# Three buffers for weight casts and residues, 4 KB runs for the up rows, and one reading of the routing table for two steps, in a hybrid decoder layer

## The chip, the cores and the metric

The kernel runs on one core of one Trainium2 chip. A core has a matrix engine (TensorE, PE in the profile; its weight loads are listed apart as PEld), a vector engine (VectorE, DVE), a scalar engine (ScalarE, ACT), GpSimd (POOL) and a queue engine (SyncE, SP). Each takes its instructions strictly in the order in which the program was built. Sixteen DMA engines move data between memory (HBM) and the on-chip buffer. The metric is the device time of one execution in microseconds (us).

## The reference, cut to what matters

One layer over 1,024 tokens of width 1,024, all in float32. First a mixer: a gated short convolution and a dilated sliding-window attention, merged by sigmoid gates. Then a retrieval of experts ("PEER"), which is most of the work:

```python
u   = rms_norm(h, norm_ffn)
q   = (u @ w_query).reshape(T, 8, 2, 128)
s   = einsum('thcd,hckd->thck', q, sub_keys)
top_s, top_i = top_k(s, 16)
...
best_s, pos = top_k(cand_s, 16)
idx   = take_along_axis(cand_i, pos, axis=-1)
gates = softmax(best_s)
...
a   = gelu(einsum('cd,ced->ce', xc, expert_down[ic]))
y   = einsum('ce,ced->cd', gc * a, expert_up[ic])
out = rms_norm(h + y, final_norm)
```

Each token picks 8 x 16 = 128 of 16,384 experts. An expert is one row of `expert_down` (for its activation) and one row of `expert_up` (what it adds).

## The kernel before, in words

Tokens stand in eight tiles of 128. The first four tiles ("half 0") go through the mixer first, then the other four ("half 1").

Tiles 0 to 3 get their experts by gathering (`experts`, the "side" work): for each of the 128 picks GpSimd issues an indirect DMA that fetches 128 rows of 4 KB (L873 from `down`, L889 from `up`), into one of four buffers `row`, and VectorE takes a dot product with the token's vector (L875) or adds the weighted row to a sum (L891). Tile 1 leaves out its `up` part, so there are 512 gathers on L873 and 384 on L889.

Tiles 4 to 7, and the `up` part of tile 1, are done densely on TensorE (`dense`): all 16,384 experts are computed in 32 groups of 512, and a routing table `g_d` in memory holds each token's gate for each expert (zero for those not picked).

- `hidden(q)`, for a group: four chunks of `down_t` go through `weights`, `project` multiplies each with the tokens, ScalarE applies Gelu (L913) into a buffer `ga` of 1 MB. Groups below `STORED` write `ga` to memory (`a_d`) and `fetch` it later; `HOLD` = 4 groups keep it on the chip.
- `build` makes the routing table: VectorE and ScalarE write one-hot matrices `oa` and `ob`, TensorE multiplies them into `psg` (L975), ScalarE copies that into `stg` (L977), and SP stores it (L981). One call covers 128 tokens.
- `weigh(q)`: loads the group's gates `gg` from `g_d` (and `gx` for tile 1), multiplies `ga` by them (L990) and splits the product into `hh` and `hl`.
- The last loop takes the groups in `order`: it loads four pieces `rawu` of the `up` rows, splits each into `uh` and `ul` (L181, L182), and multiplies. Six of ten output pieces stay in PSUM through the whole loop (`held`); the other four go through `psu` and are added to `rest` (L1089).

Every float32 product is done as three products of rounded numbers (`mm3`): a number is split into `hi` (a cast, on ScalarE) and `lo` (the residue, on VectorE), and TensorE computes hi*hi, hi*lo and lo*hi. `weights` (L161) does this for a chunk of 512 KB: a DMA into `raw`, the cast at L165 into `hi`, the residue at L167 into `lo`; `raw` has `RAWS` buffers, `hi` and `lo` have `HILO` each.

The order of the work: `main` runs the mixer of half 1 and then `dense`, both as generators that yield estimated costs; for each cost that it yields, so much of the side work is emitted, and within the first part of `dense` so much of the building of the table. A scheduler then orders each engine's instructions from readiness and that order. When the table is done, the builder's pool is closed, and the buffers of the last loop (pool `up_p`, with `uu`) take its place on the chip.

Of the kernel before, what the change touches and what calls it, by code (L numbers as in the profile page):

```python
# [8 lines left out]
F32 = mybir.dt.float32  # L9
# [4 lines left out]
ALU = mybir.AluOpType  # L14
# [3 lines left out]
P = 128  # L18
T = 1024
TH = 512  # L20
# [11 lines left out]
TC = 32  # L32
NB = 4
# [1 line left out]
PACE_D = 2.0  # L35
PACE_C = 2.2
RATE_G = 0.8
STORED = 27
HOLD = 4
RAWS = 4  # L40
HILO = 2
SUBS = ((1, 2), (1, 1))
OBUF = 4
GATES = 4
# [19 lines left out]

@with_exitstack
def hybrid_layer(ctx, tc, x, xT, pos, rotc, norm_mix, w_proj, w_v, conv_w, w_conv_out, w_attn_out,
                 gate_bias, w_out, norm_ffn, w_query, sub_keys, down, down_t, up, final_norm, out):
    nc = tc.nc
    V, S, G, PE = nc.vector, nc.scalar, nc.gpsimd, nc.tensor
    SIDE = getattr(nc, QUEUE)  # L70
# [2 lines left out]
    m8 = ctx.enter_context(tc.tile_pool(name="m8", bufs=BIGS))  # L73
    wp = ctx.enter_context(tc.tile_pool(name="wp", bufs=2))
    gt = ctx.enter_context(tc.tile_pool(name="gt", bufs=ROWS))
    ex = ctx.enter_context(tc.tile_pool(name="ex", bufs=1))
# [74 lines left out]
    s_d = dram.tile([3, P, 16, P], F32, name="s_d")  # L151
    a_d = dram.tile([STORED, P, NB, TH], F32, name="a_d")
    g_d = dram.tile([(TH + len(XT) * P) // TC, P, P, TC], F32, name="g_d")
# [26 lines left out]
    def split(hi, lo, src):  # L180
        S.copy(hi, src)  # L181
        V.tensor_tensor(lo, src, hi.bitcast(F32), op=ALU.subtract)  # L182
# [573 lines left out]
    def choose(column, last, picks):  # L756
# [50 lines left out]
        other = ex.tile([P, 16, 16], F32, tag="wk", bufs=1, name="other")  # L807
        for k in range(16):
            into = (found, other)[k % 2]
            wk = ex.tile([P, 16, 16], F32, tag="wq", bufs=2, name="wq") if k > 1 else into  # L810
            V.scalar_tensor_tensor(wk, where, float(k), names[:, :, k:k + 1].to_broadcast([P, 16, 16]),
                                   op0=ALU.is_equal, op1=ALU.mult)
            if k > 1:
                V.tensor_tensor(into, into, wk, op=ALU.add)
            if k % 2:
                yield 0.7
        V.tensor_tensor(found, found, other, op=ALU.add)
        gs = ex.tile([P, 8], F32, tag="gs", name="gs")
        ge = ex.tile([P, 8, 16], F32, tag="ge", bufs=GATES + 2, name="ge")
        V.tensor_tensor(ge, best, best[:, :, 0:1].to_broadcast([P, 8, 16]), op=ALU.subtract)  # L820
        S.activation(ge, ge, AF.Exp)
        V.tensor_reduce(gs, ge, AX.X, ALU.add)
# [77 lines left out]
    def dense():  # L900
# [8 lines left out]
        def hidden(q):  # L909
            ga = big("ga")  # L910
            for ii in range(NB):
                ps = project(weights(down_t[NB * q + ii]), U2)
                S.activation(ga[:, ii], ps, AF.Gelu)  # L913
                yield 5.3
            if q < STORED:
                nc.sync.dma_start(a_d[q], ga)
# [31 lines left out]
        def build(srcs, c0):  # L948
# [5 lines left out]
                for c in range(c0, c0 + P // TC):  # L954
# [25 lines left out]
                    for w in range(4):  # L980
                        nc.sync.dma_start(g_d[c, :, 32 * w:32 * w + 32], stg[w])  # L981

        def weigh(q):
            gg = m8.tile([P, TH // TC, NB, TC], F32, tag="big", name="gg")
            nc.sync.dma_start(gg, g_d[:TH // TC, :, NB * q:NB * q + NB].rearrange("c j i t -> j c i t"))
            ga = gas.pop(q)
            hh, hl = bigr("hh"), bigr("hl")
            for ii in range(NB):
                v = ga[:, ii].rearrange("p (c t) -> p c t", t=TC)
                V.tensor_tensor(v, v, gg[:, :, ii], op=ALU.mult)  # L990
                split(hh[:, ii], hl[:, ii], ga[:, ii])
            parts = [(hh[:, :, tt * P:tt * P + P], hl[:, :, tt * P:tt * P + P]) for tt in range(4)]
            for k in range(len(XT)):
                gx = up_p.tile([P, P // TC, NB, TC], F32, tag="gx", bufs=GXB, name="gx")
                c0 = (TH + k * P) // TC
                nc.sync.dma_start(gx, g_d[c0:c0 + P // TC, :, NB * q:NB * q + NB].rearrange("c j i t -> j c i t"))
                xh = up_p.tile([P, NB, P], F32R, tag="xh", bufs=XHB, name="xh")
                xl = up_p.tile([P, NB, P], F32R, tag="xl", bufs=XHB, name="xl")
                view = [t.rearrange("p i (c t) -> p c i t", t=TC) for t in (xh, xl)]
                S.copy(view[0], gx)  # L1000
                V.tensor_tensor(view[1], gx, view[0].bitcast(F32), op=ALU.subtract)
                parts.append((xh, xl))
            return parts
# [8 lines left out]
        for q in list(range(STORED)) + first:  # L1012
            for c in hidden(q):
                yield c / PACE_C
                debt += c * RATE_G
                while debt > 0:
                    k = next(builder, None)
# [16 lines left out]
        for n_q, q in enumerate(order):  # L1034
# [22 lines left out]
            for n in range(2):  # L1057
                uu = []
                whole = [bigr("uh_end"), bigr("ul_end")] if end and n else None
                for ii in range(0, NB, 2):  # L1060
                    raw = wp.tile([P, 2, TH], F32, tag="raw", bufs=RAWS, name="rawu")
                    r0 = (NB * q + ii) * P
                    nc.sync.dma_start(raw, up[r0:r0 + 2 * P, n * TH:n * TH + TH].rearrange("(a p) d -> p a d", a=2))
                    if whole:
                        uh, ul = (t[:, ii:ii + 2] for t in whole)
                    else:
                        uh = up_p.tile([P, 2, TH], F32R, tag="uu", bufs=UPS, name="uh")
                        ul = up_p.tile([P, 2, TH], F32R, tag="uu", bufs=UPS, name="ul")
                    split(uh, ul, raw)
                    uu.append((uh, ul))  # L1070
                for some in [[tt] for tt in range(NT)] if end and n else rounds[n]:
# [10 lines left out]
                    for tt in some:  # L1082
                        ps = acc[tt]
                        if (n, tt) in rest and not end:
                            d = rest[n, tt]
# [4 lines left out]
                        if end:  # L1090
                            st = sts[:, tt]
                            d = tokrow(h1, tt)[:, n * TH:n * TH + TH]
# [3 lines left out]
                        if end and n:  # L1096
                            V.tensor_tensor(st[:, 0:1], st[:, 0:1], st[:, 3:4], op=ALU.add)
                            r0 = TILES[tt] * P
# [14 lines left out]
    for step in main():  # L1113
        due += step
        while due > 0:
            k = next(side, None)
# [59 lines left out]
```

## Time and profile before

| | |
|---|---|
| median of 3 timed runs | 3423.3 us (3423.22 to 3426.72) |
| the profiled execution | 3433.88 us |
| its span, first to last instruction | 3432.1 us |
| PE busy | 3274.4 us (95%) |
| DVE busy | 2760.1 us (80%) |
| ACT busy | 1461.7 us (43%) |
| POOL busy | 1190.2 us (35%) |
| moved by DMA | 948.08 MB, 276 GB/s mean |

A span's busy share is a mean over stages with different limits; the stretches of the span are read one by one further down. The profiled execution is 10.6 us longer than the median of the timed runs. "Idle before" an instruction, and what ended it, is inferred from semaphore events. The full matmul has 512 columns.

### The profile page before, as it was taken

The page shows a single profiled execution, that of the slowest core. Times are in us where ns is not written, and L with a number is a line of the kernel's source. Part 1 is how long each engine was busy: PE and PEld are TensorE (multiplying, and loading weights), DVE is VectorE, ACT ScalarE, POOL GpSimd, SP SyncE. Part 2 cuts the span into 40 slices and gives each one's busy share as a digit, 9 for nine tenths or more (in the row PEclk, how much of TensorE's full clock was granted, in tenths as well). Part 3 has the DMA queues.
Part 4 walks back from the last instruction along what each step waited for, and adds up shares of the span by engine and source line. Part 5 has one row for each costly group of instructions (what it writes and reads, how often), then busy time and mean ns, then how long its engine had stood idle before and what let it go on. Part 6 is the DMA issues. An engine that isn't in the chain of part 4 may idle for free.

```text
span 3432.1 us, 47074 instructions
## 1 busy us (share of the span) xinstructions
PE 3274.4 (95%) x15923; PEld 2685.0 (78%) x15923; DVE 2760.1 (80%) x5646; ACT 1461.7 (43%) x3271; POOL 1190.2 (35%) x944
## 2 busy tenths in 40 slices
PE   7999999999989999988999989999999999999998
PEld 6787888887767777767777878888877878787787
DVE  4333355689999889988999999998887878888887
ACT  3544444443334353333226777787632222222222
POOL 0000000014543345555434443464544334444342
PEclk9999999999989999989999999999999999999999
DMA  4233335668888678988889898999989989999895
GB/s 129 77 119 110 103 127 191 244 230 305 302 279 276 227 260 307 342 316 292 315 316 328 329 330 334 344 340 336 348 301 336 334 316 338 326 340 333 309 350 208
DMA packets 364307, 948.08 MB, mean 276 GB/s; under 512 B 33952, under 2 KB 127648, under 8 KB 356640
## 3 DMA queue, kind: packets, MB, share of 16 engines
q1 hardware_dynamic: 232016, 465.27, 38.9%
q0 software_dynamic: 132048, 479.78, 38.8%
q8 instruction: 126, 2.06, 0.2%
q14 instruction: 117, 0.96, 0.1%
HBM read 843.15 MB, written 95.49 MB: 273 GB/s over the span
## 4 chain that ended last, share of the span: by engine, by line
PE 32%; DVE 20%; DMA 14%; issue 11%; POOL 5%; ACT 1%; SPq 0%; DVEq 0%; POOLq 0%; ACTq 0%
DVE row L875 6%; PE ps L178 6%; PE ps L176 6%; PE ps L177 6%; DMA row<-in_down,idx 5%; DMA rowu<-in_up,idx 4%; DMA gg<-g_d 4%; DVE lo L167 3%; POOL row L873 3%; POOL rowu L889 2%; PE held L177 2%; PE held L178 2%; PE held L176 2%; DVE acc L891 1%; PE psg L975 1%
## 5 line engine op out<-in xcount | busy, mean ns | idle before, releaser
L873 POOL DMA_INDIRECT row<-in_down,idx x512 | 640.9, 1252 | 885.2 <-DVE a L875 465.6
L889 POOL DMA_INDIRECT rowu<-in_up,idx x384 | 525.8, 1369 | 621.1 <-DVE acc L891 499.0
L165 ACT CAST hi<-raw 128x1024 fp32r<-128x1024 f32 x368 | 387.6, 1053 | 746.0 <-PE ps L177 541.1
L875 DVE CUSTOM_DVE_ANT_0 row<-row,ut 128x1024 f32<-128x1024 f32 x512 | 618.8, 1215 | 79.2 <-DMA row<-in_down,idx 74.0
L167 DVE TENSOR_TENSOR lo<-raw,hi 128x1024 fp32r<-128x1024 f32 x368 | 448.1, 1218 | 247.9 <-ACT hi L165 238.6
L178 PE MATMUL ps<-vhi,lo 128*128 128x512 f32 (+1 forms) x1408 | 535.4, 382 | 33.5 <-DVE lo L167 33.4
L176 PE MATMUL ps<-vhi,hi 128*128 128x512 f32 (+1 forms) x1408 | 530.6, 377 | 10.8 <-ACT hi L165 6.7
L891 DVE SCALAR_TENSOR_TENSOR acc<-rowu,a,acc 128x1024 f32<-128x1024 f32 x384 | 491.2, 1279 | 59.7 <-DMA rowu<-in_up,idx 57.3
L177 PE MATMUL ps<-vlo,hi 128*128 128x512 f32 (+1 forms) x1408 | 528.9, 376 | 0.0
L178 PE MATMUL ps<-uhi,lo 128*128 128x512 f32 x1024 | 409.1, 400 | 4.2 <-DVE lo L167 4.2
L176 PE MATMUL ps<-uhi,hi 128*128 128x512 f32 x1024 | 407.6, 399 | 5.7 <-ACT uhi L181 3.1
L177 PE MATMUL ps<-ulo,hi 128*128 128x512 f32 x1024 | 409.1, 400 | 0.5 <-DVE ulo L182 0.5
L178 PEld LDWEIGHTS ps<-vhi,lo 128*128 128x128 f32 x1408 | 269.1, 191 | 87.4 <-DVE lo L167 44.4
L176 PEld LDWEIGHTS ps<-vhi,hi 128*128 128x128 f32 x1408 | 269.7, 192 | 58.9 <-ACT hi L165 10.9
L177 PEld LDWEIGHTS ps<-vlo,hi 128*128 128x128 f32 x1408 | 269.1, 191 | 45.1
L177 PE MATMUL held<-ul,hh 128*128 128x512 f32 x624 | 247.0, 396 | 11.1 <-DVE ul L182 10.9
L178 PE MATMUL held<-uh,hl 128*128 128x512 f32 x624 | 244.0, 392 | 2.5 <-DVE hl L182 2.5
L176 PEld LDWEIGHTS ps<-uhi,hi 128*128 128x128 f32 x1024 | 194.1, 190 | 52.1 <-ACT uhi L181 5.2
L176 PE MATMUL held<-uh,hh 128*128 128x512 f32 x624 | 233.3, 393 | 0.0
L178 PEld LDWEIGHTS ps<-uhi,lo 128*128 128x128 f32 x1024 | 194.3, 190 | 47.9 <-DVE lo L167 6.4
L177 PEld LDWEIGHTS ps<-ulo,hi 128*128 128x128 f32 x1024 | 194.1, 190 | 45.1 <-issue 3.0
L181 ACT CAST hh<-ga 128x512 fp32r<-128x512 f32 x128 | 71.4, 618 | 353.0 <-DVE ga L990 348.9
(347 smaller groups left out, 5947.8 us busy)
## 6 DMA issues: line engine op xcount, KB each, us to landing
raw<-in_w_proj SPq DMA_DIRECT2D x128, 512.0 KB
raw<-in_down_t SPq DMA_DIRECT2D x128, 512.0 KB
rawu<-in_up SPq DMA_DIRECT2D x128, 512.0 KB
g_d<-stg SPq DMA_DIRECT2D x80, 512.0 KB
gg<-g_d SPq DMA_DIRECT2D x32, 1024.0 KB
a_d<-ga SPq DMA_DIRECT2D x27, 1024.0 KB
ga<-a_d SPq DMA_DIRECT2D x27, 1024.0 KB
raw<-in_w_query SPq DMA_DIRECT2D x48, 512.0 KB
```

The costliest lines, as they stand in the source:

```text
L165: S.copy(hi, raw)
L167: V.tensor_tensor(lo, raw, hi.bitcast(F32), op=ALU.subtract)
L176: PE.matmul(ps, l[0], r[0], start=first, stop=False)
L177: PE.matmul(ps, l[0], r[1], start=False, stop=False)
L178: PE.matmul(ps, l[1], r[0], start=False, stop=last)
L181: S.copy(hi, src)
L873: G.indirect_dma_start(out=row, out_offset=None, in_=down, in_offset=bass.IndirectOffsetOnAxis(ap=idx[:, e:e + 1], axis=0))
L875: V.tensor_tensor_reduce(out=row, in0=row, in1=ut, scale=1.0, scalar=0.0, op0=ALU.mult, op1=ALU.add, accum_out=a[:, e:e + 1])
L889: G.indirect_dma_start(out=row, out_offset=None, in_=up, in_offset=bass.IndirectOffsetOnAxis(ap=idx[:, e:e + 1], axis=0))
L891: V.scalar_tensor_tensor(acc, row, a[:, e:e + 1], acc, op0=ALU.mult, op1=ALU.add)
L975: PE.matmul(ps[:, t], ob[:, t], oa[:, t], start=True, stop=True)
```

## The change

Constants: `HILO` from 2 to 3, `RAWS` from 4 to 3, `STORED` from 27 to 28. With `STORED` = 27 the groups were taken in the order 27, 28, 29, 30, 0, 31, 1, 2, ..., and group 31's `hidden` was computed inside the last loop; with 28 it is 28, 29, 30, 31, 0, 1, 2, ..., and all 32 `hidden` are computed before the last loop. `weigh` now reads the table for two groups at once: two DMAs of 1 MB, each for half the token columns and both groups, in runs of 1 KB instead of 512 bytes; the multiplication and the split go by halves of the columns (128x1024) instead of by quarters of the group (128x512). The `up` pieces come from a second copy of the `up` matrix, `up_s`, laid out beforehand so that each partition reads one run of 4 KB (before: two of 2 KB). Two small buffers get fewer copies: `wq` 1 (was 2), `ge` 4 (was 6).

```diff
-STORED = 27
+STORED = 28
 HOLD = 4
-RAWS = 4
-HILO = 2
+RAWS = 3
+HILO = 3
...
-            wk = ex.tile([P, 16, 16], F32, tag="wq", bufs=2, name="wq") if k > 1 else into
+            wk = ex.tile([P, 16, 16], F32, tag="wq", name="wq") if k > 1 else into
...
-        ge = ex.tile([P, 8, 16], F32, tag="ge", bufs=GATES + 2, name="ge")
+        ge = ex.tile([P, 8, 16], F32, tag="ge", bufs=GATES, name="ge")
...
+        pairs = {}
+
         def weigh(q):
-            gg = m8.tile([P, TH // TC, NB, TC], F32, tag="big", name="gg")
-            nc.sync.dma_start(gg, g_d[:TH // TC, :, NB * q:NB * q + NB].rearrange("c j i t -> j c i t"))
+
+            c2 = TH // TC // 2
+            if q // 2 not in pairs:
+                both = []
+                for half in range(2):
+                    gg = m8.tile([P, c2, 2 * NB, TC], F32, tag="big", name="gg")
+                    i0 = 2 * NB * (q // 2)
+                    nc.sync.dma_start(gg, g_d[c2 * half:c2 * half + c2, :, i0:i0 + 2 * NB].rearrange("c j i t -> j c i t"))
+                    both.append(gg)
+                pairs[q // 2] = both
+            gg2 = pairs[q // 2]
             ga = gas.pop(q)
             hh, hl = bigr("hh"), bigr("hl")
-            for ii in range(NB):
-                v = ga[:, ii].rearrange("p (c t) -> p c t", t=TC)
-                V.tensor_tensor(v, v, gg[:, :, ii], op=ALU.mult)
-                split(hh[:, ii], hl[:, ii], ga[:, ii])
+            for half in range(2):
+                cols = slice(half * TH // 2, half * TH // 2 + TH // 2)
+                v = ga[:, :, cols]
+                g = gg2[half][:, :, NB * (q % 2):NB * (q % 2) + NB].rearrange("p c i t -> p i c t")
+                V.tensor_tensor(v.rearrange("p i (c t) -> p i c t", t=TC), v.rearrange("p i (c t) -> p i c t", t=TC), g,
+                                op=ALU.mult)
+                split(hh[:, :, cols], hl[:, :, cols], v)
...
-                    r0 = (NB * q + ii) * P
-                    nc.sync.dma_start(raw, up[r0:r0 + 2 * P, n * TH:n * TH + TH].rearrange("(a p) d -> p a d", a=2))
+                    nc.sync.dma_start(raw, up_s[(NB * q + ii) // 2, n])
...
+        "up_s": i["peer_up"][0].reshape(P // 2, 2, P, 2, TH).transpose(0, 3, 2, 1, 4),
```

What this does to the order of the instructions is shown at three places. The first is TensorE at the end of the building of the table: `psg` are the table's last products, `ps` those of `hidden`, `held` and `psu` those of the last loop. Before, the last `psg` stand among products of `hidden`, and 106 products of `hidden` follow before the first `held`:

```order
L178 MATMUL ps<-vhi_12766,lo 128x512
L176 MATMUL ps<-vhi_12767,hi 128x512
L177 MATMUL ps<-vlo_12769,hi 128x512
L975 MATMUL psg<-oa,ob 128x128 x8
L178 MATMUL ps<-vhi_12767,lo 128x512
L176 MATMUL ps<-vhi_12767,hi 128x512
```

After the change, at the same place:

```order
L177 MATMUL ps<-vlo_12769,hi 128x512
L178 MATMUL ps<-vhi_12767,lo 128x512
L975 MATMUL psg<-oa,ob 128x128 x8
L176 MATMUL held_22750<-uh,hh 128x512
L176 MATMUL psu<-uh,hh 128x512
L177 MATMUL held_22750<-ul,hh 128x512
```

All products of `hidden` now stand ahead of the last `psg`, and the first `held` is the next instruction; it needs the first `uh` and `hh`. 

The second place is SP's queue there. `g_d<-stg` stores a part of the table, `gg<-g_d` and `gx<-g_d` read it, `rawu` are the up rows; DMAHW and the engines' names are the semaphores waited for. Before:

```order
L981 DMA g_d<-stg 128x1024 [waits DMAHW5_49,Activation_49]
L981 DMA g_d<-stg 128x1024 [waits DMAHW6_49,Activation_49]
L1063 DMA rawu<-in_up 128x2x512 [waits DMAHW7_49,DVE_49]
L1063 DMA rawu<-in_up 128x2x512 [waits DMAHW0_49,DVE_49]
L985 DMA gg<-g_d 128x16x128 [waits DMAHW6_49,DMAHW1_49]
```

After:

```order
L981 DMA g_d<-stg 128x1024 [waits DMAHW0_49,Activation_49]
L993 DMA gg<-g_d 128x8x256
L1076 DMA rawu<-in_up_s 128x1024 [waits DMAHW2_49,DVE_49]
L981 DMA g_d<-stg 128x1024 [waits DMAHW3_49,Activation_49]
L981 DMA g_d<-stg 128x1024 [waits DMAHW4_49,Activation_49]
L981 DMA g_d<-stg 128x1024 [waits DMAHW5_49,Activation_49]
L981 DMA g_d<-stg 128x1024 [waits DMAHW6_49,Activation_49]
L993 DMA gg<-g_d 128x8x256 [waits DMAHW7_49,DMAHW6_49,DMAHW0_49]
```

The reading of the first half of the columns now stands ahead of the last four stores, which it does not need; that of the second half stands behind them.

The third place is VectorE at the end of the program. `acc` is the sum of a gathered tile (L891; at L855 it is finished), `h1b` with `held` or `psu` is the last addition for a dense tile (L1093, now L1106). Before:

```order
L891 SCALAR_TENSOR_TENSOR acc<-rowu,a,acc 128x1024 x2
L1001 TENSOR_TENSOR xl<-gx,xh 128x4x4x32
L200 TENSOR_SCALAR st<-st 128x1
L202 RECIPROCAL st<-st 128x1
L203 TENSOR_TENSOR st<-st 128x1
L204 TENSOR_TENSOR st<-st 128x1
L205 TENSOR_SCALAR st<-st 128x1
L206 TENSOR_TENSOR st<-st 128x1
L855 SCALAR_TENSOR_TENSOR acc<-acc,st,nfin 128x1024
L1093 TENSOR_TENSOR h1b_28853<-h1b_28853,held_22593 128x512
```

After:

```order
L891 SCALAR_TENSOR_TENSOR acc<-rowu,a,acc 128x1024 x2
L1106 TENSOR_TENSOR h1b_28664<-h1b_28664,held_22750 128x512
L891 SCALAR_TENSOR_TENSOR acc<-rowu,a,acc 128x1024
L1106 TENSOR_TENSOR h1b_28664<-h1b_28664,psu 128x512
L891 SCALAR_TENSOR_TENSOR acc<-rowu,a,acc 128x1024
L1106 TENSOR_TENSOR h1b_28665<-h1b_28665,psu 128x512
```

Before, all 896 gathered rows are used up ahead of the first of these additions; after, the last ten stand among and behind them.

Counts from the same orders, for all of VectorE: ahead of the 240th, 288th and 352nd residue `lo` (L167) stood 305, 417 and 569 uses of gathered rows before, and 295, 397 and 547 stand there after; ahead of the 288th `lo` stood 42 of the `oa` of the table's building, and 26 after. Ahead of the first `ul` 599 uses of gathered rows stand in both.

## Rows read from the trace of the kernel before

**Rows 1.** The page's first part: span, then busy time of each engine, its share of the span and its instructions.

```profile
span 3432.1 us, 47074 instructions
PE 3274.4 (95%) x15923; PEld 2685.0 (78%) x15923; DVE 2760.1 (80%) x5646; ACT 1461.7 (43%) x3271; POOL 1190.2 (35%) x944
```

**Rows 2.** Busy time by stretch: from and to in us, length, busy us of PE, PEld, DVE, ACT and POOL with instructions in brackets, then the granted TensorE clock as a share of full speed, the DMA engines' busy share, and GB/s. The first row is the mixer of half 0, the second the middle of the program (from there to the first `held`), the third the last loop.

```profile
0.00:640.00 640.00, 618.00 (x2951) 494.73 (x2951) 291.23 (x599) 286.91 (x549) 3.20 (x13) 1.00 0.40 132
...
640.00:2491.40 1851.40, 1744.97 (x9038) 1450.91 (x9036) 1696.71 (x4017) 939.89 (x2392) 808.45 (x636) 0.97 0.86 305
...
2491.40:3432.10 940.70, 911.41 (x3936) 739.33 (x3936) 772.20 (x1032) 234.90 (x331) 378.59 (x296) 0.99 0.88 317
```

**Rows 3.** What TensorE waited for in the middle stretch (640 to 2491.4): engine, tile and line that waited, who released it, us in total, times, longest.

```profile
PE ps L178 <- DVE lo L167: 36.5, 28, 3.6
PE ps L176 <- ACT hi L165: 11.1, 14, 2.4
...
PE pv L177 <- DVE lo L167: 8.3, 3, 4.0
```

**Rows 4.** The same view and stretch for VectorE, and two rows for ScalarE (the last from 640 to 2480).

```profile
DVE row L875 <- DMA row<-in_down,idx: 44.7, 38, 2.6
DVE lo L167 <- ACT hi L165: 42.4, 40, 5.1
DVE acc L891 <- DMA rowu<-in_up,idx: 24.6, 27, 2.4
...
ACT hi L165 <- PE ps L177: 411.6, 145, 12.9
...
ACT hi L165 <- DMA raw<-in_w_conv_out: 4.3, 2, 3.2
```

**Rows 5.** The groups by line and shape: line, engine, operation, tiles, shapes, count, then busy us and mean ns of one, then idle time before them.

```profile
L167 DVE TENSOR_TENSOR lo<-raw,hi 128x1024 fp32r<-128x1024 f32 x368 | 448.1, 1218 | 247.9 <-ACT hi L165 238.6 <-DMA raw<-in_w_proj 4.2 <-PE pst L548 2.1
...
L165 ACT CAST hi<-raw 128x1024 fp32r<-128x1024 f32 x368 | 387.6, 1053 | 746.0 <-PE ps L177 541.1 <-issue 104.3 <-PE pv L178 43.6
...
L182 DVE TENSOR_TENSOR ul<-rawu,uh 128x1024 fp32r<-128x1024 f32 x126 | 153.3, 1217 | 14.5 <-ACT uh L181 5.8 <-issue 4.3 <-PE psu L177 4.1
...
L182 DVE TENSOR_TENSOR hl<-ga,hh 128x512 fp32r<-128x512 f32 x128 | 81.2, 687 | 1.7 <-PE held L177 1.0 <-ACT hh L181 0.7
...
L990 DVE TENSOR_TENSOR ga<-ga,gg 128x512 f32<-128x512 f32 x128 | 80.2, 686 | 73.3 <-DMA gg<-g_d 73.3
```

**Rows 6.** TensorE's instructions in order of time: start, duration in us, engine, line, operation. Two of thirteen matmuls that follow one another without a gap, the first and the last.

```profile
2493.22 0.39 PE L176 MATMUL psu<-uh,hh 128*128 128x512 f32 x1
...
2495.97 0.40 PE L177 MATMUL held<-ul,xh 128*128 128x512 f32 x1
```

**Rows 7.** The same view: TensorE's last products of the table, and its first `held` (in square brackets the idle time before it and what ended it).

```profile
2463.31 1.50 PE L975 MATMUL psg<-oa,ob 128*128 128x128 f32 x12
...
2491.42 0.50 PE L176 MATMUL held<-uh,xh 128*128 128x512 f32 x1 [1.20 <-ACT xh L1000]
```

**Rows 8.** The same view of ScalarE and of SP's queue around there: the last copies into `stg`, the first cast of the last loop, the last stores of the table and the first reading of it.

```profile
2463.96 1.67 ACT L977 COPY stg<-psg 128x128 f32<-128x128 f32 x8 [2.55 <-PE psg L975]
...
2480.24 1.05 ACT L181 CAST uh<-rawu 128x1024 fp32r<-128x1024 f32 x1 [6.33 <-DMA g_d<-stg]
...
2465.14 2.54 SPq L981 DMA_DIRECT2D g_d<-stg  x4
...
2480.21 0.37 SPq L985 DMA_DIRECT2D gg<-g_d  x1
```

**Rows 9.** The same view of VectorE: two instructions of which the second does not need the first one's result, then two of which it does.

```profile
734.24 0.41 DVE L814 TENSOR_TENSOR e<-e,wq 128x256 f32<-128x256 f32 x1
734.57 0.42 DVE L814 TENSOR_TENSOR other<-other,wq 128x256 f32<-128x256 f32 x1
...
3400.73 0.16 DVE L203 TENSOR_TENSOR st<-st 128x1 f32<-128x1 f32 x1
3400.92 0.16 DVE L204 TENSOR_TENSOR st<-st 128x1 f32<-128x1 f32 x1
```

**Rows 10.** What TensorE waited for in the last loop (2491.4 to 3432.1).

```profile
PE held L177 <- DVE ul L182: 10.9, 9, 2.4
PE ps L176 <- ACT ga L913: 3.0, 1, 3.0
```

**Rows 11.** Instructions in order of time at the end: two gathers of GpSimd, and VectorE's first final addition.

```profile
3381.86 1.15 POOL L889 DMA_INDIRECT rowu<-in_up,idx  x1 [3.31 <-DVE acc L891]
...
3387.35 1.68 POOL L889 DMA_INDIRECT rowu<-in_up,idx  x1 [0.59 <-DMA rowu<-in_up,idx]
...
3402.70 0.68 DVE L1093 TENSOR_TENSOR h1b<-h1b,held 128x512 f32<-128x512 f32 x1
```

**Rows 12.** Busy time by stretch (columns as in rows 2), of single slices in the middle stretch and of one of 100 us in its last part.

```profile
1460.00:1480.00 20.00, 12.69 (x56) 10.16 (x55) 15.77 (x32) 8.55 (x17) 8.18 (x8) 0.90 0.94 339
1480.00:1500.00 20.00, 13.23 (x50) 9.97 (x51) 17.52 (x28) 4.50 (x8) 9.77 (x9) 0.59 0.87 324
...
1360.00:1380.00 20.00, 15.30 (x63) 11.31 (x63) 18.13 (x22) 9.38 (x15) 8.01 (x7) 1.00 0.95 344
1660.00:1680.00 20.00, 18.45 (x80) 14.60 (x80) 20.00 (x72) 7.04 (x9) 7.53 (x8) 1.00 0.93 330
...
2400.00:2500.00 100.00, 97.86 (x500) 82.37 (x500) 87.62 (x94) 63.42 (x183) 53.11 (x36) 1.00 0.95 348
```

More of the change, by code (lines that the diff above doesn't have):

```diff
@@ L66, in hybrid_layer @@
 def hybrid_layer(ctx, tc, x, xT, pos, rotc, norm_mix, w_proj, w_v, conv_w, w_conv_out, w_attn_out,
-                 gate_bias, w_out, norm_ffn, w_query, sub_keys, down, down_t, up, final_norm, out):
+                 gate_bias, w_out, norm_ffn, w_query, sub_keys, down, down_t, up, up_s, final_norm, out):
     nc = tc.nc
```

## The prediction

> **What bounds the kernel now.** The page's first part is read first [rows 1]: TensorE is busy for 3274.4 of 3432.1 us, so 157.7 us is all that it waits. A share over the whole span hides where, so the windows come next [rows 2]. In the first 640 us TensorE loses 22.0 us and VectorE is half idle. In the middle (640 to 2491.4) TensorE is idle for 1851.4 - 1745.0 = 106.4 us and VectorE for 154.7 us: two engines near their limit that hold each other up. In the last loop TensorE is idle for 29.3 of 940.7 us, VectorE for 168.5. So the early stage and the last loop are TensorE's own, and only the middle has a wait worth a change.
>
> The waits of the middle say which one. TensorE waits 36.5 + 8.3 us for `lo` and 11.1 us for `hi`, 55.9 us together [rows 3]. Upstream, VectorE waits 42.4 us for `hi`, and ScalarE 411.6 us until TensorE has let go of a `hi` buffer [rows 4]. That is a ring: with two buffers a weight is cast only when the one two before it is used up. One matmul follows another after (2495.97 - 2493.22) / 12 = 0.229 us [rows 6], so a weight of 24 matmuls lasts 5.5 us. Cast and residue take 1.05 + 1.22 us [rows 5], which leaves 3.2 us for all that stands ahead of `lo` on VectorE; two or three gathered rows fill that, and the waits of up to 4.0 us [rows 3] are what was over.
>
> **The change part by part.** The sum is made along TensorE, against the profiled execution of 3433.9 us; the timed median is 10.6 us shorter, and I take the same difference off at the end.
>
> *Third `hi` and `lo`.* The lead grows by one weight, 5.5 us, more than any single wait of rows 3. TensorE could win 55.9 us; at the other end 0, if VectorE is simply behind. VectorE also waits 44.7 + 24.6 us for gathered rows [rows 4], which the buffers don't shorten and which can stack up ahead of a `lo`. I take four fifths, -45, because the mean wait is short (36.5 us over 28 times is 1.3 us) and because VectorE's order now has 20 fewer uses of gathered rows ahead of the 288th `lo`.
>
> *Three `raw` instead of four.* A weight still has six places from its load to its last product, so the load stays as far ahead of its matmul, and only less ahead of its cast. ScalarE hardly waits for a weight's load in the middle (4.3 us in the costliest row [rows 4]), so 0. If starved casts became as common as residues are now, up to the gain above would be lost; that is a rival.
>
> *Group 31 ahead of the last loop.* Its 4 x 24 = 96 matmuls take 96 x 0.229 = 22.0 us. They go from the last loop into the middle: +22 there, -22 behind. The 1 MB that is now stored and fetched runs beside it; at the 348 GB/s that a busy stretch reaches [rows 12] that is 3 us each way, covered by matmuls.
>
> *The seam between the two.* Before, the table's last product ends at 2464.8 and the first `held` starts at 2491.4; 106 products of `hidden` (24.3 us) fill all but a wait of 1.2 us [rows 7]. Now none is left behind the last `psg`. The first `uh` must still wait until the last stores of the table have landed, since it takes the place of `stg`: its cast starts at 2480.24, 14.6 us after the copies to `stg` ended [rows 8]. Then come one cast of `uh` and one of `hh`, 1.05 us each. TensorE stands from 2464.8 to about 2482.3, 17.5 us, against 1.2: +16. The second reading of the table then has 46 matmuls (10.5 us) of the first half's columns as cover. Bounds: 0, if `hidden` is late anyway, and +26, if the second reading, as long as the one before (2480.2 to the first `held`), is not covered.
>
> [...]
>
> *VectorE's smaller edits.* `weigh` in pieces of 1024 instead of 512: 2 x 1.217 for 4 x 0.687 us, twice per group, 0.6 us less, 20 us over 32 groups [rows 5], all in the last loop, where VectorE is idle for 168 us: 0, and a help to `ul`. One `wq`: an instruction that needs its predecessor's result starts 0.19 us after it where one of 0.16 us would else overlap by 0.08 as the `wq` pairs do [rows 9], so 0.11 us more; 40 of 224 now stand so, 4.4 us of VectorE: 0 on TensorE. Four `ge`: the second dense tile's `ge` now follows the use of tile 1's on the same engine: 0.
>
> *Longer runs.* VectorE waits 73.3 us for `gg` [rows 5] in the last loop, and TensorE loses nothing to it there except through `ul`. GB/s per busy share is no lower in the loop that reads 512-byte and 2 KB runs (317 / 0.88 = 360) than in the first stretch (132 / 0.40 = 330) [rows 2], so I give the runs themselves 0. Rather, group 31's waits go (the 3.0 us for `ga`) and half of the 10.9 us for `ul`, plus small change [rows 10]: -10, between 0 and -20.
>
> *The end.* Ten gathered rows now stand among or behind the final additions. GpSimd issues four in 5.5 us [rows 11], 1.8 us each, so ten take 18 us from the first addition, which had 29.4 us to the end of the span [rows 11]. The tile's own finish fits into what is left, nearly: +3, between 0 and +10.
>
> Sum: middle -45 + 22 + 16 = -7, loop -22 - 10, end +3: -36. Profiled 3398, median 3387. VectorE allows the middle's part: it would win up to 42.4 us of waits for `hi` and pay 4.4 for `wq` and 4 x 1.22 for group 31's residues.
>
> **The rivals.**
> *The table becomes last (slower).* VectorE is full in slices where TensorE is at 92% (1660 to 1680, [rows 12]), and the order puts 16 more `oa` behind the 288th `lo`. If VectorE paces the building, the waits for `lo` come back as waits for `psg`: nothing is won, the middle costs +22 + 16, the loop gives -22 - 5, the end +6: +17, 3440. Against it speak the 42.4 us that VectorE itself waits for `hi`. It decides as soon as fewer than about 9 of the 55.9 us go.
> *The DMA engines hold the loop.* The loop moves 317 GB/s x 940.7 us = 298 MB; 32 us less asks for 328. If gathers and up rows don't come faster, the 22 us of group 31 turn into waits for `ul`: 3387 + 24 = 3411. Slices of 348 GB/s speak against it, the long waits for rows for it.
> *Starved casts.* With three `raw` half of the 45 us and the small gains are eaten by waits for loads: about 3387 + 22 + 10 = 3419. The few waits of now speak against it.
> *All of it.* The full 55.9 us, some 12 us of the 3% that the middle's clock lacks [rows 2], a loop without idle time (-20) and a free end: 3387 - 11 - 12 - 10 - 3 = 3351.
>
> **How the numbers follow.** Chances: forecast 0.45 (3370 to 3402), table last 0.16, DMA 0.15, starved casts 0.08, all of it 0.16. The range runs from 3350 to 3432: it takes in the best case and the two middle ones and leaves out most of the slower one. A measurement here tells 0.2% (7 us) from no change. Faster gets the forecast, the best case, and most of the DMA and casts cases: 0.74; no change the rest of those: 0.10; slower the table's: 0.16.
>
> **What would show it.** Right: TensorE's waits for `lo` and `hi` in the middle fall from 55.9 to some 11 us and VectorE's for `hi` to under 10; one wait of 15 to 20 us at the first `held`, put down to ScalarE's cast or a store of the table; no products of `hidden` after it; a loop of about 905 us from the first `held`. Wrong: new waits of `psg` on VectorE, waits of `hi` on loads of `raw`, a loop still over 925 us, or final additions that wait for gathered rows.

## The result and the profile after

The changed kernel takes 3399.1 us (median of 5 runs, 3394.9 to 3402.5); the kernel before took 3426.7 beside it. The ratio is 0.992 with a 95% interval of 0.9902 to 0.9938: faster by 0.6 to 1.0%, where 3387 us was forecast and 3350 to 3432 allowed. The profiled execution took 3402.5 us, 31.4 less than that of before. Each trace below is one execution, and executions of one kernel lie up to 30 us apart (the kernel before beside the first four experiments: 3411.8 to 3442.1), so a difference of some 10 us between stretches of two traces isn't told from that scatter; verdicts rest on the medians.

The page's first part of the changed kernel:

```profile
span 3400.7 us, 46783 instructions
PE 3250.1 (96%) x15923; PEld 2683.8 (79%) x15923; DVE 2756.8 (81%) x5518; ACT 1460.1 (43%) x3205; POOL 1207.3 (36%) x944
```

TensorE's instructions are as many as in [rows 1]; its idle time went from 157.7 to 150.6 us, and 24 us of its busy time went too. Where the 31.4 us lie is shown by the windows (columns as in [rows 2]): the middle to the first `held`, the last loop, then two short stretches around the seam.

```profile
640.00:2499.60 1859.60, 1747.08 (x9139) 1463.89 (x9138) 1702.13 (x4018) 942.54 (x2398) 785.94 (x633) 0.97 0.86 306
2499.60:3400.70 901.10, 885.24 (x3840) 723.69 (x3840) 763.00 (x905) 231.07 (x261) 418.66 (x299) 0.99 0.91 332
2480.00:2500.00 20.00, 4.16 (x17) 3.87 (x18) 10.63 (x10) 5.68 (x20) 10.17 (x8) 0.50 0.90 328
2500.00:2510.00 10.00, 9.43 (x28) 7.00 (x28) 10.00 (x9) 4.90 (x6) 5.04 (x3) 0.64 1.05 365
```

The middle is 8.2 us longer than in [rows 2], the loop 39.6 us shorter. All the gain lies behind the first `held`.

What TensorE waited for in the middle (columns as in [rows 3]):

```profile
PE ps L178 <- DVE lo L167: 17.7, 15, 2.3
PE held L176 <- ACT hh L181: 15.2, 1, 15.2
PE pst L716 <- ACT hi L165: 11.4, 1, 11.4
PE ps_t L952 <- DVE name L939: 8.2, 1, 8.2
PE psg L975 <- ACT stg L977: 8.1, 8, 3.8
PE psg L975 <- DVE ob L968: 7.7, 4, 5.1
```

The waits of `ps` for `lo` are halved, and those for `hi`, 11.1 us in [rows 3], fall to 0.2. Other waits grow by more than the 37 us that the weights lose. Before, two of them were:

```profile
PE pst L716 <- DVE u L707: 10.3, 4, 9.3
PE psg L975 <- ACT stg L977: 5.9, 1, 5.9
```

With all their releasers, `psg` (the table's products) went from 8.5 to 22.1 us, `pst` (the transposes of `u` at the end of the mixer) from 18.6 to 26.3 and `ps_t` (transposes for the table) from 1.4 to 8.2. The 11.4 us that the view puts down to a `hi` end at 1457.5, when VectorE has just written the `u` that this `pst` reads; before, the longest wait for `u`, 9.3 us, stood at the same place in TensorE's order. Only the wait of the first `held` was forecast. The same stretch for VectorE and ScalarE:

```profile
DVE row L875 <- DMA row<-in_down,idx: 50.4, 42, 4.0
DVE lo L167 <- ACT hi L165: 33.4, 40, 3.9
DVE acc L891 <- DMA rowu<-in_up,idx: 28.1, 21, 3.0
...
ACT hi L165 <- PE ps L177: 263.6, 106, 7.5
ACT hi L165 <- DMA raw<-in_down_t: 95.1, 23, 8.2
```

VectorE's three rows are the key to the result. Their sum before was 44.7 + 42.4 + 24.6 = 111.7 us [rows 4]; now it is 50.4 + 33.4 + 28.1 = 111.9. It waits 9 us less for `hi` and 9 us more for gathered rows. On ScalarE the shift is larger: 148 us less waiting until TensorE lets a `hi` go, 95 us more for loads of `raw`.

The seam in order of time, TensorE first: the table's last products, the first `held`, two matmuls right behind it and two a little later; then SP's last stores and ScalarE's first two casts.

```profile
2480.59 3.78 PE L975 MATMUL psg<-oa,ob 128*128 128x128 f32 x16 [3.75 <-ACT stg L977]
2499.62 0.80 PE L176 MATMUL held<-uh,hh 128*128 128x512 f32 x1 [15.24 <-ACT hh L181]
...
2500.64 0.63 PE L177 MATMUL held<-ul,hh 128*128 128x512 f32 x1
2501.07 0.63 PE L177 MATMUL psu<-ul,hh 128*128 128x512 f32 x1
...
2508.14 0.39 PE L177 MATMUL held<-ul,hh 128*128 128x512 f32 x1
2508.37 0.39 PE L178 MATMUL held<-uh,hl 128*128 128x512 f32 x1
...
2484.70 3.17 SPq L981 DMA_DIRECT2D g_d<-stg  x4
...
2497.58 1.04 ACT L181 CAST uh<-rawu 128x1024 fp32r<-128x1024 f32 x1 [12.39 <-DMA g_d<-stg]
2498.53 1.04 ACT L181 CAST hh<-ga 128x1024 fp32r<-128x1024 f32 x1
```

The cast of `uh` waits for the last stores of the table, as worked out: 15.24 us without a product. The granted clock is 0.50 from 2480 to 2500. Then matmuls of 512 columns follow one another in 2501.07 - 2500.64 = 0.43 us until 2507, at a granted clock of 0.50 from 2500 to 2507; from there it is 2508.37 - 2508.14 = 0.23 us, at 0.95 from 2507 to 2510. The 16 slow ones cost 16 x 0.20 = 3.2 us.

Waits in the loop from 2500.5 to the end, the longest of TensorE and one row of VectorE:

```profile
PE held L178 <- DVE hl L182: 0.6, 1, 0.6
...
DVE ga L1003 <- DMA gg<-g_d: 26.6, 14, 4.3
```

TensorE's 10.9 us for `ul` [rows 10] are down to 0.5, and two thirds of VectorE's 73.3 us for `gg` [rows 5] are gone here; 8.8 us of them now stand ahead of the first `held`. The end, on VectorE: the first final addition and the last gathered row.

```profile
3364.24 0.68 DVE L1106 TENSOR_TENSOR h1b<-h1b,held 128x512 f32<-128x512 f32 x1
...
3383.32 1.29 DVE L891 SCALAR_TENSOR_TENSOR acc<-rowu,a,acc 128x1024 f32<-128x1024 f32 x1 [0.41 <-DMA rowu<-in_up,idx]
```

From the first addition to the end of the span it is 36.5 us now, 29.4 before [rows 11].

### The profile page after: what moved, and what is told of

Read it like the earlier page. It is cut to its first block, busy times and chain, and to the rows that moved or that the text cites. A ratio compares the mean times of both kernels' runs of the same rounds, so it can differ in the third digit from the quotient of the medians.

```text
span 3400.7 us, 46783 instructions
## 1 busy us (share of the span) xinstructions
PE 3250.1 (96%) x15923; PEld 2683.8 (79%) x15923; DVE 2756.8 (81%) x5518; ACT 1460.1 (43%) x3205; POOL 1207.3 (36%) x944
## 4 chain that ended last, share of the span: by engine, by line
PE 63%; DVE 15%; DMA 13%; issue 5%; ACT 2%; POOL 1%; SPq 0%; DVEq 0%; ACTq 0%; POOLq 0%
PE ps L176 10%; PE ps L177 10%; PE ps L178 10%; DMA row<-in_down,idx 5%; PE held L177 5%; PE held L176 5%; PE held L178 5%; DVE row L875 4%; PE psu L176 3%; PE psu L177 3%; PE psu L178 3%; DVE lo L167 3%; PE psg L975 2%; DMA rowu<-in_up,idx 2%; PE sc L467 2%
## 5 line engine op out<-in xcount | busy, mean ns | idle before, releaser
L873 POOL DMA_INDIRECT row<-in_down,idx x512 | 650.8, 1271 | 868.1 <-DVE a L875 485.1
L889 POOL DMA_INDIRECT rowu<-in_up,idx x384 | 532.9, 1388 | 607.6 <-DVE acc L891 488.8
L167 DVE TENSOR_TENSOR lo<-raw,hi 128x1024 fp32r<-128x1024 f32 x368 | 448.9, 1220 | 228.5 <-ACT hi L165 224.5
L178 PE MATMUL ps<-vhi,lo 128*128 128x512 f32 (+1 forms) x1408 | 527.0, 376 | 15.8 <-DVE lo L167 15.8
L891 DVE SCALAR_TENSOR_TENSOR acc<-rowu,a,acc 128x1024 f32<-128x1024 f32 x384 | 490.8, 1278 | 51.0 <-DMA rowu<-in_up,idx 48.8
L176 PE MATMUL held<-uh,hh 128*128 128x512 f32 x624 | 232.8, 395 | 15.2 <-ACT hh L181 15.2
L181 ACT CAST uh<-rawu 128x1024 fp32r<-128x1024 f32 x126 | 131.3, 1048 | 223.2 <-PE psu L178 151.9
```

The lines of the kernel that those rows point to most:

```text
L167: V.tensor_tensor(lo, raw, hi.bitcast(F32), op=ALU.subtract)
L176: PE.matmul(ps, l[0], r[0], start=first, stop=False)
L178: PE.matmul(ps, l[1], r[0], start=False, stop=last)
L873: G.indirect_dma_start(out=row, out_offset=None, in_=down, in_offset=bass.IndirectOffsetOnAxis(ap=idx[:, e:e + 1], axis=0))
L889: G.indirect_dma_start(out=row, out_offset=None, in_=up, in_offset=bass.IndirectOffsetOnAxis(ap=idx[:, e:e + 1], axis=0))
L891: V.scalar_tensor_tensor(acc, row, a[:, e:e + 1], acc, op0=ALU.mult, op1=ALU.add)
```

## The experiments

Ratios are to the kernel before, timed beside each of these kernels.

**The buffers alone, on the kernel before.**

```diff
-RAWS = 4
-HILO = 2
+RAWS = 3
+HILO = 3
...
-            wk = ex.tile([P, 16, 16], F32, tag="wq", bufs=2, name="wq") if k > 1 else into
+            wk = ex.tile([P, 16, 16], F32, tag="wq", name="wq") if k > 1 else into
...
-        ge = ex.tile([P, 8, 16], F32, tag="ge", bufs=GATES + 2, name="ge")
+        ge = ex.tile([P, 8, 16], F32, tag="ge", bufs=GATES, name="ge")
```

> The kernel before with the buffer edits alone (HILO 3, RAWS 3, one wq, four ge). Theory 1 (the third hi and lo win about 37 us of waits for lo and hi in the middle, and the open seam and casts that wait for loads give most of it back): the time is 5 to 20 us under before; waits of TensorE for lo and hi from 640 us to the first held fall from 55.9 to about 20 us; the order has no product of hidden behind the last psg, so one wait of about 15 us stands at the first held; waits of hi on loads of raw rise from about 5 us to over 80. Theory 2 (the buffers are neutral or cost time, the gain comes from the last loop alone): same time or slower, with the first held at least 15 us later than before.

3447.6 us, ratio 1.0054 (1.0037 to 1.0071): slower. The middle by windows, and TensorE's waits in it:

```profile
640.00:2507.20 1867.20, 1742.47 (x9058) 1461.28 (x9056) 1706.08 (x4023) 939.14 (x2393) 807.61 (x637) 0.96 0.86 304
```

```profile
PE held L176 <- ACT xh L1000: 24.7, 1, 24.7
PE psg L975 <- ACT stg L977: 20.6, 12, 7.6
PE ps L178 <- DVE lo L167: 13.1, 11, 2.6
```

Theory 2 holds: the time is longer and the first `held` comes 15.8 us later. The waits for `lo` and `hi` do fall as theory 1 said, from 55.9 to 16.3 us, and others take their place. On the kernel before the buffers shorten nothing.

**wq and ge alone, on the kernel before** (the last two of the three edits above).

> The kernel before with one wq and four ge only. Theory 1, these cost 40 x 0.11 us of VectorE and nothing on TensorE: ratio to before 0.998 to 1.002. Theory 2, part of what the buffer edits cost (20 us in e1) is theirs, since ge of the second dense tile must wait or the chain of wq holds up the table: ratio 1.003 or above.

3422.1 us, ratio 0.9996 (0.9985 to 1.0007). The middle:

```profile
640.00:2485.50 1845.50, 1738.87 (x9040) 1448.23 (x9038) 1690.09 (x4006) 941.17 (x2393) 797.07 (x626) 0.98 0.86 304
```

The small edits cost nothing; the loss of the first experiment belongs to `HILO` and `RAWS`.

**Group 31 alone.**

```diff
-STORED = 27
+STORED = 28
```

> The kernel before with STORED 28 alone. Theory 1 (group 31's 96 matmuls fill idle time of the middle): the loop from the first held is 22 us shorter, the first held comes 5 to 15 us later, the time is 7 to 17 us under before; 200 products of hidden stand behind the last psg, so there is no wait at the first held. Rival (the middle has no room, as the sum on record priced it): first held 22 us later, time the same within 5 us.

3410.6 us, ratio 0.995 (0.9929 to 0.9972). Middle and loop by windows:

```profile
640.00:2501.70 1861.70, 1766.20 (x9136) 1471.16 (x9135) 1711.86 (x4033) 947.75 (x2404) 820.67 (x640) 0.97 0.87 308
2501.70:3409.00 907.30, 885.27 (x3841) 723.03 (x3839) 757.43 (x1016) 225.51 (x319) 381.81 (x291) 0.99 0.90 323
```

Theory 1 holds: the time is 16 us shorter. The middle grows by 10.3 us, though 96 matmuls (22.0 us) came in, and the loop gives 33.4, more than the 22 expected. TensorE's idle time in the middle falls from 106.4 to 95.5 us: part of the group is computed in it.

**Group 31 and the table read for two groups at once** (the change's `weigh`, nothing else).

> The kernel before with STORED 28 and the reading of the table for two groups, buffers and up rows as before. Theory 1 (the pairs free VectorE of its waits for gg, which made ul late): VectorE's waits for gg in the loop fall from 73 to under 35 us, TensorE's waits for ul from 11 to under 3, and the time is 8 to 15 us under that of STORED 28 alone. Rival (those waits were beside the path): within 5 us of STORED 28 alone.

3396.9 us, ratio 0.9898 (0.9858 to 0.9939).

```profile
640.00:2504.10 1864.10, 1764.28 (x9132) 1469.73 (x9131) 1708.02 (x4026) 943.79 (x2399) 805.25 (x639) 0.97 0.87 307
2504.10:3394.10 890.00, 880.57 (x3841) 721.89 (x3840) 751.68 (x894) 229.80 (x260) 418.28 (x292) 1.00 0.90 330
```

The reading in pairs takes another 17.3 us off the loop, and 13.7 us off the median, inside the range of theory 1; with four runs the interval of this ratio just touches that of group 31 alone. TensorE's waits for `ul` are gone, and VectorE's for `gg` fall to 38.8 us, not quite the 35 expected. These two edits by themselves reach the time of the whole change; the intervals overlap.

**The up rows in 4 KB runs alone.**

```diff
-                    r0 = (NB * q + ii) * P
-                    nc.sync.dma_start(raw, up[r0:r0 + 2 * P, n * TH:n * TH + TH].rearrange("(a p) d -> p a d", a=2))
+                    nc.sync.dma_start(raw, up_s[(NB * q + ii) // 2, n])
```

> The kernel before with the 4 KB runs of the up rows alone. Theory 1 (runs are worth nothing): the same within 5 us, TensorE's waits for ul in the loop stay near 11 us. Rival (the 2 KB runs were what made ul late): waits for ul fall under 4 us, the time 8 us or more under before.

3423.2 us, ratio 0.9988 (0.9964 to 1.0012): no difference that can be told. TensorE's waits for `ul` are 7.5 us, so the rival's sign (under 4) did not come.

**The whole change without the buffers.**

```diff
-RAWS = 3
-HILO = 3
+RAWS = 4
+HILO = 2
```

> The changed kernel with HILO back at 2 and RAWS back at 4 (wq, ge, pairs, the up rows' runs and STORED 28 as changed). Theory 1, the gain lies in the last loop and the buffers give nothing of their own: 3388 to 3398 us, no longer than the changed kernel's 3399; TensorE's waits for lo and hi in the middle are back at 40 to 55 us, the first held follows without a long wait, the loop from there takes about 890 us (890.0 with STORED and the pairs alone, 901.1 in the changed kernel). Theory 2, within the full change the third hi and lo are worth what was forecast, some 20 us or more net of the seam: 3420 us or above.

3406.5 us, ratio 0.9954 (0.9936 to 0.9972): between the two theories, nearer to the first. The windows, then VectorE's waits in the middle:

```profile
640.00:2489.50 1849.50, 1757.04 (x9136) 1465.19 (x9135) 1697.89 (x4013) 947.49 (x2400) 797.20 (x627) 0.98 0.86 306
2489.50:3400.40 910.90, 880.98 (x3841) 720.92 (x3839) 766.26 (x907) 228.85 (x259) 428.77 (x304) 0.99 0.90 330
```

```profile
DVE lo L167 <- ACT hi L165: 53.1, 51, 4.3
DVE row L875 <- DMA row<-in_down,idx: 44.3, 43, 3.1
DVE acc L891 <- DMA rowu<-in_up,idx: 18.7, 15, 4.4
```

The middle is 10.1 us shorter than with the buffers, not longer, and VectorE's three rows sum to 116.1 us. The loop is 9.8 us longer than in the changed kernel, and that lies at its end: the first final addition stands at 3350.2, 50.2 us ahead of the end of the span, since 17 instead of 10 gathered rows stand behind it in VectorE's order (4 in the kernel of the pairs, with 31.3 us). So the third `hi` and `lo`, with one `raw` less, moved 7 gathered rows from the end into the middle (599 instead of 592 stand ahead of the first `ul`). In the two profiled executions both shifts cancel (spans of 3400.7 and 3400.4 us). The medians differ by 0.3%, where the two intervals just meet; no trace shows where that lies.

**The seam covered.**

```diff
-RATE_G = 0.8
+RATE_G = 0.9
```

> The changed kernel with RATE_G 0.9 instead of 0.8: the table's building is emitted a little sooner, and 96 products of hidden stand between the last psg and the first held instead of none. Theory 1, the uncovered seam costs its wait of 15.2 us and some 4 us of half clock after it: the wait falls below 4 us, time 3378 to 3386. Theory 2, the wait only stands where VectorE and ScalarE are behind anyway, and covering it moves it to psg, ps_t or lo: 3393 to 3405, with first held no earlier than 2492.

3394.2 us, ratio 0.9907 (0.9888 to 0.9927), not told apart from the changed kernel. The middle, and a TensorE wait in it that grew:

```profile
640.00:2500.70 1860.70, 1754.37 (x9145) 1469.80 (x9143) 1707.41 (x4024) 944.70 (x2398) 811.89 (x637) 0.97 0.87 307
```

```profile
PE psg L975 <- DVE ob L968: 17.3, 4, 8.4
```

The wait of the first `held` falls from 15.2 to 1.8 us, and the first `held` comes no earlier (2500.7 against 2499.6). Theory 2 holds: in place of the 13.4 us, `psg` waits 9.6 us longer for `ob`, which VectorE writes, and `ps` 3.1 longer for `lo`. The loop is 4.5 us shorter; the granted clock is 1.00 from 2400 to 2500 and from 2500 to 2800, where the changed kernel has 0.90 and 0.99.

**Three raw beside two hi and lo** (the whole change with `HILO` 2).

> The changed kernel with HILO back at 2, RAWS left at 3: the weights have one place less from load to last product than before. Theory 1, starved casts cost little since ScalarE mostly waits for a hi buffer to be let go: ScalarE's waits for loads of raw below 60 us, time within 8 us of the version with RAWS 4 (e5). Theory 2, the loads, not the buffers of hi and lo, set the pace with three raw: TensorE's waits for lo and hi rise by 15 us or more over e5's, time 12 us or more above it.

3416.2 us, ratio 0.9975 (0.9963 to 0.9986), 9.7 us above the version with four: just above the 8 us of theory 1, below the 12 of theory 2. The middle:

```profile
640.00:2518.10 1878.10, 1772.23 (x9159) 1476.02 (x9158) 1721.27 (x4033) 945.77 (x2402) 820.68 (x641) 0.97 0.87 307
```

TensorE's waits for `lo` and `hi` rise by 17 us, as theory 2 said, but ScalarE hardly waited for loads here (12 us), so starved casts are not the cause. The middle is 28.6 us longer with 23.4 us more work of VectorE in it: 607 instead of 592 gathered rows stand ahead of the first `ul`. The end is shorter. Which of the orders' differences makes the time stays open.

This run also prices the third `hi` and `lo` where three `raw` are given: the changed kernel has them and is 0.6% faster than this one (0.992 against 0.9975, the intervals apart), with 8 rows fewer in the middle, which is 18.5 us shorter.

**Two raw beside three hi and lo** (the changed kernel with `RAWS` 2).

> The changed kernel with RAWS 2 (HILO 3): five places from a weight's load to its last product, as in e7, but shared out the other way. Theory 1, what counts is the sum of the places: e7's 3416 again, 3408 to 3424 us, with more starved casts than the changed kernel's 129 us. Theory 2, the places of hi and lo count and the load's do not: 3393 to 3404. A third outcome, above 3430, would say that the last loop needs three raw for the up rows.

3451.0 us, ratio 1.0081 (1.0051 to 1.0111). Neither theory: the time is above 3430, but it lies in the middle (1902.6 us), while the loop takes 904.0. ScalarE's waits there:

```profile
ACT hi L165 <- DMA raw<-in_down_t: 150.3, 60, 7.1
ACT hi L165 <- PE ps L177: 134.7, 48, 8.8
```

With two, casts wait longer for loads of `down_t` alone than for buffers, and TensorE's waits for `hi` are back (17.4 us). So the places of the load count by themselves, and not only their sum with those of `hi` and `lo`.

**The memory spent on gathered rows instead.** First the version without the buffers, with

```diff
-ROWS = 4
+ROWS = 5
```

> The version of e5 (changed kernel with HILO 2, RAWS 4) with ROWS 5 instead of 4: the 4 KB per partition that the change spends on hi, lo and raw go to a fifth buffer for gathered rows. Theory 1, in the middle the residues stand behind gathered rows on VectorE, so the lead of the gathers is what is short: VectorE's waits for gathered rows in the middle fall from 62 to 90 us in the versions with four to below 40, TensorE's waits for lo and hi below 25, time 3370 to 3390 us. Theory 2, the rows come no faster, since GpSimd's issuing and the DMA engines limit them and not the buffers: 3397 to 3412 us, waits as in e5.

3443.3 us, ratio 1.0051 (1.0031 to 1.0071): slower than both theories. The middle, and VectorE's waits in it:

```profile
640.00:2553.60 1913.60, 1779.85 (x9134) 1483.55 (x9133) 1761.25 (x4078) 952.70 (x2406) 869.67 (x683) 0.96 0.87 311
```

```profile
DVE lo L167 <- ACT hi L165: 82.3, 74, 4.2
DVE row L875 <- DMA row<-in_down,idx: 22.0, 24, 2.5
...
DVE acc L891 <- DMA rowu<-in_up,idx: 2.9, 4, 1.2
```

The rows do come in time now, as theory 1 said: 24.9 us of waits instead of 63.0. But VectorE's waits for `hi` rise from 53.1 to 82.3, the sum of the three rows is 107.2, and its idle time in the middle is 152.4 us against 151.6. In its order 640 instead of 592 gathered rows now stand ahead of the first `ul`, and the middle carries 63.4 us more of VectorE's work and is 64.1 us longer. The last loop gives little back: TensorE is busy for 881.0 us in it in both versions, and only the end gets shorter (50.2 to 31.4 us).

Then six, beside `RAWS` 3 and `HILO` 2:

> The version of e7 (HILO 2, RAWS 3) with ROWS 6: as much on-chip memory as the changed kernel, all of it on gathered rows. Theory 1 (gathers' lead is short): at least 15 us below e7's 3416, and the raw buffer that is given up costs its 10 us against e9. Theory 2 (rows come no faster): 3408 to 3424 us, as e7.

3481.7 us, ratio 1.0164 (1.014 to 1.0189). The same, further on:

```profile
640.00:2584.60 1944.60, 1805.93 (x9165) 1494.83 (x9165) 1791.50 (x4129) 953.57 (x2407) 922.29 (x709) 0.96 0.87 314
```

668 gathered rows stand ahead of the first `ul`, and VectorE's idle time in the middle is 153.1 us once more.

**Three buffers for rows** (the changed kernel with `ROWS` 3), the same thing the other way round.

> The changed kernel with ROWS 3 instead of 4 and nothing else. In VectorE's order 958 instead of 983 uses of gathered rows then stand ahead of the first ul, and 38 instead of 10 behind the first final addition. Theory 1, the middle is as long as VectorE's own work in it plus some 155 us: 25 uses less at 1.28 us, so the first held at 2462 to 2476 instead of 2499.6, VectorE busy for 32 us less there; the end grows by the rows left over, at 1.8 us each, so the whole stands at 3390 to 3415. Theory 2, the middle hangs on TensorE's weights and on rows that come late: with three buffers VectorE waits longer for rows, the first held comes at 2495 or later, the whole at 3420 or above.

3647.9 us, ratio 1.0658 (1.0621 to 1.0695). Theory 2 holds in each of its signs, though its bounds were far below this. (The expectation's 958 and 983 count two instructions for each row of `down`; in rows it is 574 and 599.) VectorE's work in the middle does fall, by 22.1 us, as theory 1 said, but its idle time rises to 289.2 us.

```profile
640.00:2609.20 1969.20, 1790.15 (x9151) 1489.43 (x9149) 1680.03 (x3994) 943.12 (x2400) 736.64 (x607) 0.96 0.81 282
```

```profile
DVE row L875 <- DMA row<-in_down,idx: 134.2, 86, 5.5
DVE acc L891 <- DMA rowu<-in_up,idx: 85.7, 47, 5.1
```

With three, 219.9 us of the middle go to rows that are late. The middle is 109.6 us longer than in the changed kernel, the loop up to the first final addition 69.6 us, and the end, with 38 rows behind that addition, 68.7 us. So "VectorE's work plus 155 us" is no law of the kernel; it holds where the rows have four buffers or more and the loads three `raw` or more (with two `raw` the idle time is 169.9 us).

## Why the prediction was right, and where it was not

The direction was right. That the time came only 12 us above the forecast is luck: two errors of 15 us had opposite signs. Along the profiled executions: the middle was forecast at -7 and came out at +8.2; from the first `held` to the first final addition, -32 was forecast, and 911.3 us became 864.6, -46.7; the end, +3 forecast, +7.1 found. Together -31.4, where -36 stood. The other 7 of the 12 us come from the last step: 10.6 us were taken off from profiled to timed, and the changed kernel's profiled execution lies only 3.4 above its median.

*Third `hi` and `lo`, -45: the step that failed.* Its first half held: the weights' waits for `lo` and `hi`, 55.9 us, fell to 18.8. What failed is that they were counted as time. The middle with the buffers is 10.1 us longer than without (1859.6 against 1849.5), and on the kernel before 21.7 us longer (1867.2 against 1845.5, each with the small edits). The loss lies behind the transposes of `u`, where the table is built (14.3 and 17.3 us), and is about what the wait at the first `held` grew by; but with that wait covered (the `RATE_G` run) the middle is no shorter. By the medians the third `hi` and `lo` and the `raw` given up for them are worth 0.3% within the change and cost 0.6% on the kernel before. The prediction's check, that VectorE "would win up to 42.4 us of waits for `hi`", left out that VectorE takes residues and gathered rows in one order: it came to the rows earlier and waited there. Its three waits sum to 107 to 116 us in every version with four or five row buffers and three or more `raw`, and its idle time in the middle lies between 150 and 161 us in them. So the middle is as long as VectorE's own work in it plus some 155 us, and that work goes with the gathered rows ahead of the first `ul`:

| version | gathered rows ahead of the first `ul` | VectorE busy in the middle, us | length of the middle, us |
|---|---|---|---|
| without the buffers | 592 | 1697.9 | 1849.5 |
| the changed kernel | 599 | 1702.1 | 1859.6 |
| three `raw`, two `hi` and `lo` | 607 | 1721.3 | 1878.1 |
| five buffers for rows | 640 | 1761.3 | 1913.6 |
| six buffers for rows | 668 | 1791.5 | 1944.6 |

TensorE's own waits then land where VectorE's work is next due: `psg`, `pst`, `ps_t`, the first `held`. That is the mechanism of the rival "the table becomes last", which named `psg` and VectorE; its 3440 did not come, as group 31 cost little and the loop gave more. That fewer waits of one kind come with more of the other is shown by the runs (fewer for `hi` with the buffers, fewer for rows with five of those, the sum nearly the same); that the order on VectorE is the reason is argued from the traces. No run changed the buffers and kept the order of the instructions, so what the buffers do by themselves and what the changed order does stay mixed.

*Three `raw`, 0.* Half right. Casts starved as the rival said, for 95.1 us in the one row shown and 129 us with those of three other weights, while the weights' products wait 0.2 us for `hi`; so nearly all of it seems to have been off the path. Three `hi` and `lo` beside four `raw`, which would show it, were not run. With two `hi` and `lo` the fourth `raw` is worth 9.7 us, and two `raw` show where it ends.

*Group 31, +22 in the middle.* Mis-sized: 10.3 us alone, and 4.0 between the versions with and without it that have neither buffer (1849.5 against 1845.5, the pairs and runs included). It was priced as if TensorE were full; 92 to 107 us of idle time were there to take it.

*The seam, +16.* The wait was 15.2 instead of 17.5 us, by the mechanism given. As a term of the sum it is wrong all the same: covered, it gives the middle nothing. The granted clock was 0.50 over the wait, and the 16 matmuls 0.43 us apart right behind it cost 3.2 us, for which the sum has no term. The 12 us that the best case adds for the clock of the middle no run shows: it is 0.97 there in both kernels, 0.96 to 0.98 in the experiments.

*The loop.* The 22 us of group 31 came (-35.7 from the first `held` to the first final addition in the run of group 31 alone, waits for `ul` included). The reading in pairs was mis-sized: it took 875.6 us to 858.7 there, 13.7 us of the median, where "-10, between 0 and -20" stood for it and all small change together. The rival of the DMA engines did not come: the shorter loop moves 332 GB/s at a busy share of 0.91, and TensorE's waits for `ul` went instead of growing. The longer runs and the smaller edits were right at 0: no difference could be told, within 0.4% and 0.2%.

*The end, +3.* Mis-sized by 4 us. The ends go with the rows left behind the first final addition: 29.4 to 31.5 us with none, 31.3 with 4, 36.5 with 10, 50.2 with 17.

Of the signs of being right, that of the first `held` came, that of the waits for `lo` and `hi` in the main (18.8 us where some 11 stood), and the loop took 901 us where about 905 stood. VectorE's wait for `hi` stayed at 33 us where less than 10 was to show the lead at work. Two of the signs of being wrong came as well: `psg` waits 7.7 us for VectorE's `ob` (1.9 before), and `hi` waits for loads of `raw`. These three told against the -45.

## What to carry to other kernels

When two kinds of work share an engine that runs in order, a buffer that ends the waits of one kind pays only if the other kind isn't late next (here VectorE waited 9 us less for `hi` and 9 us more for rows): add up that engine's waits over both before counting the gain. A wait removed from the engine that waits is time only if the engine that releases it gets further ahead too: the `RATE_G` run took 13.4 us off the wait of the first `held`, which came 1.1 us later. More buffers can also slow a kernel through a scheduler that uses them to pull other work forward: a fifth for rows put 48 more of them ahead of the first `ul` and made the middle 64.1 us longer.

## What was not expected of the hardware and the program

A buffer more for gathered rows made the kernel slower by about 1% (3443.3 against 3406.5 us) though the waits for rows fell from 63.0 to 24.9 us, and one less than in the changed kernel made it slower by 7% (3647.9 against 3399.1): four lies between two losses of different kinds. Covering a wait of 15 us, with 16 matmuls 0.43 instead of 0.23 us apart behind it, moved the whole by 5 us, within what the runs can tell.
